# Eight heads of a gated delta network on one core: the turn of each head's result goes from TensorE to VectorE blocks and DRAM transfers

## The chip, the core and the metric

The kernel runs on one core of a Trainium2 chip. The metric is the device time of one execution in microseconds (us). Three runs of the kernel before took 2697.6, 2695.23 and 2692.07 us, median 2695.23.

## The reference, cut to what matters

One layer of a decoder: a prompt of 2048 tokens and 32 sample tokens, width 1024, all in float32. Of the two branches the change touches the second, a gated delta rule with 8 heads of 128 features:

```
h = layernorm(x) * (1 + scale) + shift
u_a, v_a, z_a, qkv, z_b, b_raw, a_raw, ga, gb = split(h @ w_in)
y_a   = chunk_gmlp(gelu(u_a), gelu(v_a), z_a, ...)        # branch A
q,k,v = split(silu(short_conv(qkv)))                      # branch B, per head
o, s  = gated_delta(l2norm(q), l2norm(k), v, g, beta, s0) # chunks of 64/128 tokens, a state S carried along
o     = rmsnorm(o) * onorm_g                              # over the 128 features of a head
y_b   = o * silu(z_b)
m     = sigmoid(ga) * (y_a @ w_pa) + sigmoid(gb) * (y_b @ w_pb)
x_new = layernorm(ALPHA * x + gate * (m @ w_o))           # gate comes from silu(c) @ w_ada
```

## The kernel before, in words

**Tiling.** The prompt goes in two halves of 1024 tokens (half 0 carries the sample tokens too). Each float32 product is made of three matmuls of split operands (high and low parts), so a group of 128 output features by 384, 288 or 512 tokens takes 24 matmuls. In each half the groups follow one another on TensorE: a small one for b and a, then per head k, q, v, z_b (and ga for the first six heads), then gb (8 groups), V (8), U and Z (16), the rest of ga, PA, PB and w_o. In half 1, V is made with tokens on the partitions (`v_tokens`): its weights go, split, into the eight Y tiles, which the heads use as buffers until then. `v_take` waits for the event `("headdone", 1, 7)`, the end of the last head, and then takes all of them.

**Side work of a head.** Beside the groups run, per head: the convolutions and norms of k, q and v, a Gram matrix, an inverse of unit triangular blocks (`inverse`, mostly GpSimd), a chain of 8 steps over the state (`chain`), and `o_out`, once for each 512 tokens (q = 0, 1). `o_out` takes the chain's result from PSUM with tokens on the partitions, works out its norm (ScalarE squares, a power on GpSimd), multiplies it into the buffer `ob` (VectorE), turns it by four TensorE transposes of 128x128 into PSUM (`pt`), multiplies it by gain and silu(z_b), which stand with features on the partitions (VectorE), and writes it to DRAM (`d_yb`).

**What sets the order.** A greedy planner in Python (`Sched`) runs when the program is built. Every piece of work is a stream that asks for an engine with a modelled duration, for a buffer of a role, or for an event; the planner takes the stream with the earliest modelled start and writes its instruction down. So the order on every engine is fixed before the run, and each engine works through its own list in order. All transfers go through one queue, SP. In the model a transfer ends at the earliest 2 us after its start, and longer with many short runs; consecutive `dma` calls in one stream that pass `dep=t` follow one another in the model.

**Buffers.** A head's small buffer `hs` and its `ZZ` have two copies; `chain` gives them back when both `("oq", half, h, q)` have been signalled, so head h+2 can start its k only after head h's last `d_yb` write. The inverse takes the role `Z`, two units of scratch, for three arrays Z1, Z2, Z3. In half 0 the gate of the layer (`ada_gate`) loads eight blocks of `w_ada` of 512 KB into buffers of the role `gw`, which lie in the same Y tiles as the heads' buffers, splits each into Y2R or Y3R in turn (ScalarE and VectorE) and multiplies it (six matmuls 9x512 each).

Of the kernel before, what the change touches and what calls it, by code (L numbers as in the profile page):

```python
# [13 lines left out]
P = 128  # L14
D = 1024
KT = 8
H = 8
# [152 lines left out]
def hybrid_step_kernel(ctx: ExitStack, tc: tile.TileContext, x_prompt, x_sample, state_conv, state_ssm,  # L170
# [15 lines left out]
    def const(n):  # L186
        o = cpos[0]
        cpos[0] += (n + 1) // 2 * 2
        assert cpos[0] <= NF, cpos[0] - NF
        return o  # L190
# [14 lines left out]
    def place(off):  # L205
        if off >= RO:
            return AR, off - RO, NF - RO
        if off >= WHL:
            return TW_, off - WHL, 4096
        if off >= YO:  # L210
            return ycur[(off - YO) // YT], (off - YO) % YT, YT
        return TX, off, 32 * UNIT
    PS = ps_pool.tile([P, 8, 512], F32, name="psum")[:]

    def V(off, *dims, p0=0, np_=P):
        dims = [[1, d] if isinstance(d, int) else list(d) for d in dims]
        t, o, st = place(off)
        return bass.AP(t.tensor, t.offset + p0 * st + o, [[st, np_]] + dims)

    def Q(bank, off, *dims, p0=0, np_=P):  # L220
        dims = [[1, d] if isinstance(d, int) else list(d) for d in dims]
        return bass.AP(PS.tensor, PS.offset + p0 * 4096 + bank * 512 + off, [[4096, np_]] + dims)

    def dram(name, n):
        return dr_pool.tile([1, n], F32, name=name)[:]

    def DV(t, off, *dims):
        return bass.AP(t.tensor, t.offset + off, [list(d) for d in dims])
# [3 lines left out]
    def role(name, cands):  # L232
        roles[name] = cands

    def xs_units(base, first, n):
        return tuple(range(base + first, base + first + n))
# [5 lines left out]
    def Yc(first, n):  # L242
        return (YO + first * UNIT, xs_units(32, first, n))

    def Rc(first, n):
        return (RO + first * UNIT, xs_units(64, first, n))
# [3 lines left out]
    role("KV", [Yc(16, 4), Yc(20, 4)])  # L250
    role("ZZ", [Yc(24, 2), Yc(26, 2)])
    role("U", [Yc(28, 2)])
    role("Z", [Yc(30, 2)])
    role("cp", [Rc(0, 2), Rc(2, 2)])
    role("cu", [Rc(4, 1)])
    role("kx", [Rc(5, 1)])
# [60 lines left out]
    S = Sched(98 + len(unit_names), roles)  # L317
# [11 lines left out]
    c_ong, c_negA, c_dtb = const(2), const(8), const(8)  # L329
# [10 lines left out]
    def SCR(**kw):  # L340
        return V(c_scr, P // 2, **kw).bitcast(BF16)
# [18 lines left out]

    d_v = {(half, h, i): dram(f"d_v{half}{h}{i}", n * P)
           for half, ns in enumerate(((384, 384, 256), (512, 512))) for h in range(H) for i, n in enumerate(ns)}


    def fsz(ap):
        n = 1
        for s in ap.shape[1:]:
            n *= s
        return n
# [7 lines left out]
    def dma(out, in_, dep=None, late=0.0):  # L377
        n = 1
        for s in out.shape:
            n *= s  # L380
        run = 4 * min(out.shape[-1], in_.shape[-1])
        t = yield ("o", "DMA", (n * 4 / 300.0 * max(1.0, 512.0 / run), late), dep)
        nc.sync.dma_start(out=out, in_=in_)
        return t

    def act(out, in_, func=AF.Copy, dep=None, scale=None, bias=None, accum=None):
        ns = fsz(out) / 1.2 + (55 if in_ps(in_) else 95)
        ns += 93 * (not isinstance(scale, (int, float, type(None)))) + 93 * (bias is not None) + 150 * (accum is not None)
        if func in (AF.Ln, AF.Exp, AF.Tanh, AF.Gelu_apprx_tanh):
            ns += 1300 * ((func == AF.Ln) != S.ln_table)  # L390
            S.ln_table = func == AF.Ln
        t = yield ("o", "ACT", ns, dep)
        kw = {}
        if scale is not None:
            kw["scale"] = scale
        if bias is not None:
            kw["bias"] = bias
        if accum is not None:
            kw["accum_out"] = accum
        nc.scalar.activation(out, in_, func, **kw)  # L400
        return t

    def dve_ns(out, ins, rate=1.0):
        return fsz(out) / (0.96 * rate) + (80 if any(in_ps(i) for i in ins) else 130)

    def tt(out, a, b, op, dep=None, eng="DVE"):
        if eng == "DVE":
            t = yield ("o", "DVE", dve_ns(out, (a, b)), dep)
            nc.vector.tensor_tensor(out=out, in0=a, in1=b, op=op)  # L409
        else:  # L410
            t = yield ("o", "POOL", 240 + 2.15 * fsz(out), dep)
            nc.gpsimd.tensor_tensor(out=out, in0=a, in1=b, op=op)  # L412
        return t
# [8 lines left out]
    def stt(out, a, s, b, op0, op1, dep=None):  # L422
        aps = not isinstance(s, (int, float))
        t = yield ("o", "DVE", dve_ns(out, (a, b)) + 60 * aps, dep)
        nc.vector.scalar_tensor_tensor(out=out, in0=a, scalar=s, in1=b, op0=op0, op1=op1)  # L425
        return t

    def vtrans(out, a, dep=None):

        t = yield ("o", "DVE", fsz(out) / 0.96 + 150, dep)  # L430
        nc.vector.transpose(out, a)  # L431
        return t
# [19 lines left out]
    def tp(out, in_, idn=None, dep=None):  # L452
        t = yield ("o", "PE", 109.0, dep)
        nc.tensor.transpose(out, in_, ident[: in_.shape[0], : in_.shape[0]] if idn is None else idn)  # L454
        return t
# [697 lines left out]
    def hd(half, h):  # L1153
        return heads.setdefault((half, h), {})
# [268 lines left out]
    def inverse(half, h, t):  # L1423
        me = hd(half, h)
# [3 lines left out]
        t = max(t, t0)  # L1428
# [9 lines left out]
        t = yield ("o", "DVE", 210.0, ub[2])  # L1438
        nc.vector.tensor_copy(V(T, 256), V(c_ti, 256))
        t = max(t, tw)  # L1440
        for j in range(31):
# [5 lines left out]
            t = yield from tt(tmp, arow, piv, ALU.mult, dep=t, eng=SUB)  # L1447
            t = yield from tt(dst, dst, tmp, ALU.subtract, dep=t, eng=SUB)
        S.release(wb, t)
        for cls in range(4):  # L1450
# [5 lines left out]
        t = yield ("o", "DVE", 340.0, tw)  # L1456
# [7 lines left out]
                           dep=max(tw, Ub[2]))  # L1464
# [4 lines left out]
                           bc(V(c_bd, [32, 2], [1, 32], **h64).unsqueeze(1), [64, 8, 2, 32]), ALU.mult, dep=max(t, t0))  # L1469

        Zb = yield ("a", "Z")
        Z1, Z2, Z3 = (Zb[0] + 256 * i for i in range(3))
        B = [dict(p0=32 * i, np_=32) for i in range(4)]


        pb = yield ("a", "pt")
        pc = yield ("a", "pu")
        t = yield ("o", "PE", 16 * 38.0 + 120, max(t, pb[2], pc[2], Zb[2]))
# [6 lines left out]
        t = yield ("o", "PE", 24 * 32.0 + 120, max(ta, tb))  # L1485
        for c in range(8):
            nc.tensor.matmul(Q(pb[0], 32 * c, 32, **B[1]), V(Uc + 32 * c, 32, **B[1]), V(Z1 + 32 * c, 32, **B[1]),  # L1487
                             start=True, stop=True)
            for a, q in ((2, pc), (0, pb)):
# [3 lines left out]
                           dep=max(t, t2))  # L1493
# [10 lines left out]
        pb = yield ("a", "pt")  # L1504
        t = yield ("o", "PE", 16 * 32.0 + 140, max(ta, pb[2]))
        for c in range(8):
# [5 lines left out]
                           dep=tc_)  # L1512
        t = yield from act(V(Z2, 256), Q(pb[0], 0, 256), dep=t)
        pc = yield ("a", "pu")
        t = yield ("o", "PE", 16 * 32.0 + 140, max(t, t3, pc[2]))
        for c in range(0, 8, 2):
            i = 64 * (c // 2)
# [6 lines left out]
        t = yield from ts(V(U + P + 64, [2 * P, 4], [1, 64], **h64), Q(pc[0], 0, [64, 4], [1, 64], **l64), -1.0,  # L1524
                          ALU.mult, dep=max(t, tb))
        S.release(pb, ta)
        S.release(pc, t)
        t = max(ta, t)
# [63 lines left out]
    def o_out(half, h, q, po, t):  # L1592
        me = hd(half, h)
        hs = me["hs"][0]
        te = t
        for i in range(4):
            t = yield from act(SCR(), Q(po[0], i * P, P), AF.Square, accum=V(hs + 56 + 4 * q + i, 1), dep=te)
        tn = 0.0
        for cgi in range(len(CG[half])):
            tn = max(tn, (yield ("w", ("nq", half, h, cgi))))  # L1600
        no, rs = V(hs + 56 + 4 * q, 4), V(hs + 64 + 4 * q, 4)
        t = yield from stt(no, no, 1.0 / P, V(hs + 48 + 4 * q, 4), ALU.mult, ALU.add, dep=max(t, tn))
        t = yield from pow_(rs, no, 0)
        ob = yield ("a", "ob")
        t = yield from tt(V(ob[0], [P, 4], [1, P]), Q(po[0], 0, [P, 4], [1, P]), bc(rs.unsqueeze(2), [P, 4, P]),
                          ALU.mult, dep=max(t, ob[2]))
        S.release(po, t)
        pb = yield ("a", "pt")
        for i in range(4):
            t = yield from tp(Q(pb[0], i * P, P), V(ob[0] + i * P, P), dep=max(t, pb[2]))  # L1610
        tz = 0.0
        for cgi in range(len(CG[half])):
            tz = max(tz, (yield ("w", ("zz", half, h, cgi))))
        t = yield from stt(V(ob[0], 512), Q(pb[0], 0, 512), V(c_ong, 1), V(me["ZZ"][0] + 512 * q, 512),
                           ALU.mult, ALU.mult, dep=max(t, tz))
        S.release(pb, t)
        t = yield from dma(DV(d_yb, h * P * TW + 512 * q, [TW, P], [1, 512]), V(ob[0], 512), dep=t)
        S.release(ob, t)
        S.signal(("oq", half, h, q), t)
        S.signal(("ybd", half, h, q), t + 500)  # L1620
# [568 lines left out]
    for half in range(2):  # L2189
# [54 lines left out]
        for cgi in range(len(CG[half]) if half == 0 else 1):  # L2244
            for g in range(KT):
# [3 lines left out]
                elif g > 1:  # L2249
                    keep = (XO + 4 * g * UNIT, lambda: ("done", last[(0, "pb")]), (P, TW))  # L2250
                q = add(w_o, D, g * P, half, P, hy, (lambda k, c, half=half: ("m", half, k, c)), o_sink(half, g), 1.0,
                        cgs=[cgi], pre=after_pb if cgi == 0 and g == 0 else None, keep=keep,
                        use=wo[g] if cgi else None)
# [81 lines left out]
```

## Time and profile before

| what | value |
|---|---|
| runs | 2697.6, 2695.23, 2692.07 us, median 2695.23 |
| profiled execution, its own time | 2690.44 us |
| its span in the trace | 2688.7 us |
| TensorE busy | 2641.5 us, 98% of the span |
| VectorE, ScalarE, GpSimd busy | 1479.2, 987.0, 555.9 us |
| transfers | 281.34 MB in 506976 packets |
| mean granted TensorE clock | 0.996 |

The page gives for each engine its busy time; 98% for TensorE says that the kernel is a nearly gapless row of matmuls. In the views below PE is TensorE, DVE is VectorE, ACT is ScalarE, POOL is GpSimd and SP is the queue that issues the transfers. "L449" is a line of the kernel; the same helper lines stand three lines lower (L452) in the changed one.

### The profile page before, as it was taken

How to read it: one execution, taken by the hardware profiler on the slowest of the kernel's cores; microseconds unless marked ns; L12 is line 12 of the kernel's file. 1: busy time of each engine (PE TensorE's matmuls, PEld its weight loads, DVE VectorE, ACT ScalarE, POOL GpSimd, SP SyncE). 2: the span in 40 equal slices, each digit the busy share in tenths (PEclk: the TensorE clock that was granted, in tenths of full speed). 3: DMA queues.
4: the chain of work that ended last, by engine and by line, in shares of the span. 5: the costliest groups of instructions: out<-in, count | busy, mean ns of one | idle time of the engine just before them, and what ended most of it. 6: DMA issues, size and time to landing. Idle time of an engine off the chain costs nothing. (4 is left out here: it accounts for less than half of the span.)

```text
span 2688.7 us, 43893 instructions
## 1 busy us (share of the span) xinstructions
PE 2641.5 (98%) x16250; PEld 2331.7 (87%) x16250; DVE 1479.2 (55%) x3247; ACT 987.0 (37%) x2650; POOL 555.9 (21%) x1452
## 2 busy tenths in 40 slices
PE   6999999999999999999999999999999999999998
PEld 4999989999899999999997788888888888888876
DVE  5676767777643364334547666666762323433446
ACT  5554545455332222221325444444442312221120
POOL 2054544334300000000001434444350000000001
PEclk9999999999999999999999999999999999999999
DMA  6232343333675462332523333333233322233332
GB/s 217 69 91 74 102 110 90 87 82 82 174 193 109 101 202 71 101 118 83 164 78 108 83 88 94 93 85 92 73 80 101 113 92 77 77 116 98 111 121 86
DMA packets 506976, 281.34 MB, mean 105 GB/s; under 512 B 210025, under 2 KB 471457, under 8 KB 506762
## 3 DMA queue, kind: packets, MB, share of 16 engines
q1 hardware_dynamic: 506762, 278.55, 36.9%
q8 instruction: 127, 2.08, 0.3%
q14 instruction: 87, 0.71, 0.1%
HBM read 210.03 MB, written 68.43 MB: 104 GB/s over the span
## 5 line engine op out<-in xcount | busy, mean ns | idle before, releaser
L449 PE MATMUL psum<-TX,TWHL 128*128 128x384 f32 (+3 forms) x9296 | 1959.4, 359 | 9.3 <-DVE TX L409 5.9
L449 PEld LDWEIGHTS psum<-TX,TWHL 128*128 128x128 f32 (+1 forms) x9296 | 1556.3, 188 | 163.8 <-DVE TX L409 7.0
L400 ACT ACTIVATE arena<-psum 128x128 bf16<-128x128 f32 (+9 forms) x888 | 299.4, 346 | 719.7 <-PE psum L449 596.8
L438 POOL TENSOR_TENSOR arena<-arena 128x4 f32<-128x4 f32 (+4 forms) x139 | 121.2, 874 | 1592.3 <-DVE arena L419 1380.7
L425 DVE SCALAR_TENSOR_TENSOR arena<-arena 128x512 f32<-128x512 f32 (+9 forms) x633 | 348.9, 560 | 91.2 <-ACT arena L400 79.6
L412 POOL TENSOR_TENSOR arena<-arena 128x60 f32<-128x60 f32 (+24 forms) x992 | 352.1, 355 | 174.7 <-DMA d_v<-arena 36.9
L409 DVE TENSOR_TENSOR TWHL<-arena,TWHL 128x512 fp32r<-128x512 f32 (+1 forms) x344 | 233.2, 687 | 198.3 <-ACT TWHL L400 196.1
L425 DVE SCALAR_TENSOR_TENSOR arena<-arena,psum 128x128 f32<-128x128 f32 (+3 forms) x342 | 132.7, 404 | 357.2 <-PE psum L449 246.6
L400 ACT ACTIVATE TWHL<-arena 128x512 fp32r<-128x512 f32 x344 | 213.6, 627 | 240.3 <-PE psum L449 117.0
L400 ACT ACTIVATE arena<-arena 128x128 f32<-128x128 f32 (+9 forms) x513 | 234.7, 493 | 130.4 <-DVE arena L425 86.2
L409 DVE TENSOR_TENSOR arena<-arena 128x1024 f32<-128x1024 f32 (+12 forms) x251 | 108.6, 438 | 9.6 <-DMA arena<-in_lnv_g_dram 5.6
L454 PE MATMUL psum<-arena 128*128 128x128 f32 (+8 forms) x381 | 93.6, 269 | 2.6 <-ACT Y3F L400 0.8
L400 ACT ACTIVATE Y7F<-psum 32x256 f32<-32x256 f32 (+6 forms) x115 | 46.5, 405 | 117.8 <-DVE Y7F L431 37.5
L1226 POOL COPY arena<-arena 128x3 f32<-128x3 f32 x120 | 37.4, 312 | 233.2 <-ACT arena L400 232.8
L425 DVE SCALAR_TENSOR_TENSOR arena<-psum,arena 128x512 f32<-128x512 f32 (+4 forms) x72 | 36.9, 528 | 84.2 <-PE psum L449 84.0
L400 ACT ACTIVATE TX<-arena 128x512 fp32r<-128x512 f32 (+2 forms) x84 | 46.9, 586 | 89.3 <-DMA arena<-d_yb 72.2
L400 ACT ACTIVATION_READ_ACCUMULATOR arena<-psum 128x1 f32 x392 | 76.5, 195 | 0.0
L419 DVE TENSOR_SCALAR arena<-arena 128x3 f32<-128x3 f32 (+8 forms) x247 | 54.4, 224 | 36.3 <-ACT arena L400 24.2
L449 PEld LDWEIGHTS psum<-arena 128*128 128x128 f32 (+3 forms) x364 | 55.2, 171 | 17.1 <-issue 7.0
L454 PEld LDWEIGHTS psum<-arena 128*128 128x128 f32 (+8 forms) x381 | 49.7, 136 | 22.8 <-issue 12.0
L449 PE MATMUL psum<-arena 128*128 128x128 f32 (+5 forms) x364 | 66.5, 269 | 1.2 <-ACT arena L400 1.0
L409 DVE TENSOR_TENSOR TX<-arena,TX 128x512 fp32r<-128x512 f32 (+2 forms) x84 | 52.1, 639 | 21.7 <-ACT TX L400 21.5
(249 smaller groups left out, 2706.2 us busy)
## 6 DMA issues: line engine op xcount, KB each, us to landing
arena<-in_w_in_dram SPq DMA_DIRECT2D x288, 256.0 KB
out_dram<-arena SPq DMA_DIRECT2D x25, 512.0 KB
arena<-in_x_prompt_dram SPq DMA_DIRECT2D x24, 512.0 KB
arena<-d_gc SPq DMA_DIRECT2D x16, 512.0 KB
arena<-d_blk SPq DMA_DIRECT2D x64, 128.0 KB
d_yb<-arena SPq DMA_DIRECT2D x32, 256.0 KB
d_vh<-arena SPq DMA_DIRECT2D x16, 512.0 KB
arena<-d_vh SPq DMA_DIRECT2D x16, 512.0 KB
```

What stands on the lines that cost most here:

```text
L400: nc.scalar.activation(out, in_, func, **kw)
L409: nc.vector.tensor_tensor(out=out, in0=a, in1=b, op=op)
L412: nc.gpsimd.tensor_tensor(out=out, in0=a, in1=b, op=op)
L419: nc.vector.tensor_scalar(out=out, in0=a, scalar1=s1, scalar2=s2, op0=op0, **kw)
L425: nc.vector.scalar_tensor_tensor(out=out, in0=a, scalar=s, in1=b, op0=op0, op1=op1)
L438: nc.gpsimd.tensor_tensor(out=out, in0=a, in1=e, op=ALU.pow)
L449: nc.tensor.matmul(out, lhsT, rhs, start=start, stop=stop)
L454: nc.tensor.transpose(out, in_, ident[: in_.shape[0], : in_.shape[0]] if idn is None else idn)
L1226: nc.gpsimd.tensor_copy(V(c_tail + gi, [24, 3]), V(x0 + n0, 3))
```

## The change: o_out of every head but the last of half 1

For 30 of the 32 calls of `o_out` (all but half 1, head 7), the four TensorE transposes are replaced. VectorE transposes `ob` within blocks of 32x32 into a new buffer `obt` (one instruction, 128x512); four transfers of 64 KB write the four bands of 32 partitions to a new DRAM array `d_o`, in runs of 128 B, so that block (i, j) lands at place (j, i); a fifth transfer of 256 KB reads it back into `ob`. The multiplication by gain and z_b then takes its first operand from `ob` in place of PSUM. The unit for `obt` is the second one of the role `Z`; Z1 and Z2 of the inverse now share a place.

```diff
-    role("Z", [Yc(30, 2)])
+    role("Z", [Yc(30, 1)])
+    role("obt", [Yc(31, 1)])
...
+    d_o = {(half, h, q): dram(f"d_o{half}{h}{q}", 512 * P) for half in range(2) for h in range(H) for q in range(2)}
...
-        Z1, Z2, Z3 = (Zb[0] + 256 * i for i in range(3))
+        Z1, Z2, Z3 = Zb[0], Zb[0], Zb[0] + 256
...
         S.release(po, t)
-        pb = yield ("a", "pt")
-        for i in range(4):
-            t = yield from tp(Q(pb[0], i * P, P), V(ob[0] + i * P, P), dep=max(t, pb[2]))
         tz = 0.0
         for cgi in range(len(CG[half])):
             tz = max(tz, (yield ("w", ("zz", half, h, cgi))))
-        t = yield from stt(V(ob[0], 512), Q(pb[0], 0, 512), V(c_ong, 1), V(me["ZZ"][0] + 512 * q, 512),
+        src, pb = V(ob[0], 512), None
+        if (half, h) == (1, H - 1):
+            pb = yield ("a", "pt")
+            src = Q(pb[0], 0, 512)
+            for i in range(4):
+                t = yield from tp(Q(pb[0], i * P, P), V(ob[0] + i * P, P), dep=max(t, pb[2]))
+        else:
+
+            bt = yield ("a", "obt")
+            t = yield from vtrans(V(bt[0], 512), src, dep=max(t, bt[2]))
+            d = d_o[half, h, q]
+            for i in range(4):
+                t = yield from dma(DV(d, 32 * i, [512, 32], [P, 4], [32 * 512, 4], [1, 32]),
+                                   V(bt[0], [P, 4], [32, 4], [1, 32], p0=32 * i, np_=32), dep=t)
+            S.release(bt, t)
+            t = yield from dma(src, DV(d, 0, [512, P], [1, 512]), dep=t)
+        t = yield from stt(V(ob[0], 512), src, V(c_ong, 1), V(me["ZZ"][0] + 512 * q, 512),
                            ALU.mult, ALU.mult, dep=max(t, tz))
-        S.release(pb, t)
+        if pb is not None:
+            S.release(pb, t)
         t = yield from dma(DV(d_yb, h * P * TW + 512 * q, [TW, P], [1, 512]), V(ob[0], 512), dep=t)
```

Since the planner works from these durations, the change also moves instructions elsewhere. At three places the order reads as follows.

TensorE at the end of the heads of half 1, before: `psum<-TX,TWHL` are matmuls of the projections (here of gb), `psum<-arena,Y5F` and `Y3F` the last links of head 7's chain, `psum<-arena` at L454 the four transposes of its last `o_out`, and `Y0R,TX` is where `v_tokens` begins.

```order
L449 MATMUL psum<-TX,TWHL 128x512 x4
L449 MATMUL psum<-arena,Y5F 128x128
L449 MATMUL psum<-arena,Y3F 128x128
L449 MATMUL psum<-TX,TWHL 128x512 x19
L454 MATMUL psum<-arena 128x128
L449 MATMUL psum<-TX,TWHL 128x512 x3
L454 MATMUL psum<-arena 128x128
L449 MATMUL psum<-TX,TWHL 128x512 x3
L454 MATMUL psum<-arena 128x128
L449 MATMUL psum<-TX,TWHL 128x512 x3
L454 MATMUL psum<-arena 128x128
L449 MATMUL psum<-TX,TWHL 128x512 x96
L449 MATMUL psum<-Y0R,TX 128x512 x3
```

The same place in the changed kernel:

```order
L452 MATMUL psum<-TX,TWHL 128x512 x4
L452 MATMUL psum<-arena,Y7F 128x128
L452 MATMUL psum<-arena,Y5F 128x128
L452 MATMUL psum<-arena,Y3F 128x128
L457 MATMUL psum<-arena 128x128 x4
L452 MATMUL psum<-Y0R,TX 128x512 x3
```

The 124 matmuls of gb that stood between the chain's last link and `v_tokens` now all stand ahead of the chain's end; only the four transposes are left between the two.

TensorE in the V stage of half 0, before (`Y2R,Y4R` and `Y3R,Y4R` with 9x512 are `ada_gate`'s matmuls, one buffer each; the others are V's projections):

```order
L449 MATMUL psum<-TX,TWHL 128x384 x18
L449 MATMUL psum<-Y3R,Y4R 9x512
L449 MATMUL psum<-TX,TWHL 128x384 x3
L449 MATMUL psum<-Y3R,Y4R 9x512
L449 MATMUL psum<-TX,TWHL 128x384 x3
```

and the part of the changed kernel where they stand closest:

```order
L452 MATMUL psum<-TX,TWHL 128x384 x9
L452 MATMUL psum<-Y3R,Y4R 9x512 x6
L452 MATMUL psum<-Y2R,Y4R 9x512 x3
L452 MATMUL psum<-TX,TWHL 128x384 x3
...
L452 MATMUL psum<-TX,TWHL 128x384 x15
L452 MATMUL psum<-Y3R,Y4R 9x512 x6
L452 MATMUL psum<-Y2R,Y4R 9x512 x6
L452 MATMUL psum<-Y3R,Y4R 9x512 x4
L452 MATMUL psum<-TX,TWHL 128x288 x3
```

Before, three or four projection matmuls stood between two of the gate's, and 18 to 31 between two buffers; now buffers follow one another with none between.

ScalarE at the same place in the changed kernel (`Y2R<-Y5F` and `Y3R<-Y5F` are the high parts of the gate's weights, `Y7F<-psum` the gelu of V, `TWHL<-arena` the split of the next projection weights, `Y0F` and `Y1F` normalise token rows of half 1):

```order
L403 ACTIVATE Y1F<-Y1F,arena 128x1024
L403 ACTIVATE Y2R<-Y5F 128x1024
L403 ACTIVATE Y3R<-Y5F 128x1024
L403 ACTIVATE TWHL<-arena 128x512 x2
L403 ACTIVATE Y2R<-Y5F 128x1024
L403 ACTIVATE Y7F<-psum 128x384
L403 ACTIVATE Y3R<-Y5F 128x1024
L403 ACTIVATE Y0F<-Y0F,arena 128x1024
L403 ACTIVATE Y2R<-Y5F 128x1024
L403 ACTIVATE Y1F<-Y1F,arena 128x1024
L403 ACTIVATE Y3R<-Y5F 128x1024
```

All eight splits now stand behind the first gelu of V; before, six of them stood ahead of it and two behind.

## Rows read from the trace of the kernel before

**Rows 1.** The page's head and its parts 1 and 2: the span, busy time and share of each engine, and busy tenths in 40 slices of 67.2 us (TensorE).

```profile
span 2688.7 us, 43893 instructions
PE 2641.5 (98%) x16250; PEld 2331.7 (87%) x16250; DVE 1479.2 (55%) x3247; ACT 987.0 (37%) x2650; POOL 555.9 (21%) x1452
...
PE   6999999999999999999999999999999999999998
...
```

**Rows 2.** Busy time of each engine in stretches (from:to, length, then PE, PEld, DVE, ACT, POOL, granted clock, share and rate of transfers). 200:820 is the heads of half 0, gb and the start of V; 820:1200 the rest of V, U and Z; 1560:2100 the heads of half 1 and gb.

```profile
200.00:820.00 620.00, 619.10 (x4672) 574.57 (x4671) 423.20 (x1080) 290.68 (x938) 231.57 (x625) 1.00 0.42 111
820.00:1200.00 380.00, 377.04 (x2342) 372.07 (x2341) 158.81 (x308) 92.94 (x186) 6.29 (x10) 1.00 0.43 117
1560.00:2100.00 540.00, 539.07 (x3431) 444.68 (x3430) 318.91 (x664) 242.13 (x732) 200.44 (x518) 1.00 0.33 89
```

**Rows 3.** The view of waits, TensorE, from 60 us to the end: what it waited for, us in total, times, longest.

```profile
PE psum L449 <- DVE TX L409: 6.9, 3, 5.2
PE psum L449 <- ACT Y7F L400: 2.4, 1, 2.4
```

**Rows 4.** Timeline of TensorE at the end of head 7, half 1 (start us, length, instruction, count; in square brackets idle time before it).

```profile
2072.86 0.39 PE L449 MATMUL psum<-arena,Y3F 128*128 128x128 f32 x2
2073.01 4.69 PE L449 MATMUL psum<-TX,TWHL 128*128 128x512 f32 x19
2077.53 0.27 PE L454 MATMUL psum<-arena 128*128 128x128 f32 x1
2077.56 0.94 PE L449 MATMUL psum<-TX,TWHL 128*128 128x512 f32 x3
2078.34 0.27 PE L454 MATMUL psum<-arena 128*128 128x128 f32 x1
...
2079.98 22.64 PE L449 MATMUL psum<-TX,TWHL 128*128 128x512 f32 x96
2102.46 0.86 PE L449 MATMUL psum<-Y0R,TX 128*128 128x512 f32 x3
```

**Rows 5.** Timeline of VectorE after the chain's end in half 1: the last `o_out` (2076.17 and 2080.26) and the low parts of `v_tokens`' weights (Y0R to Y7R).

```profile
2076.17 0.69 DVE L409 TENSOR_TENSOR arena<-psum,arena 128x512 f32<-128x512 f32 x1 [1.12 <-POOL arena L438]
2080.26 0.75 DVE L425 SCALAR_TENSOR_TENSOR arena<-psum,arena,Y6F 128x512 f32<-128x512 f32 x1 [3.40 <-PE psum L454]
2082.13 0.28 DVE L409 TENSOR_TENSOR Y0R<-arena,Y0R 128x128 fp32r<-128x128 f32 x1
...
2098.91 0.29 DVE L409 TENSOR_TENSOR Y7R<-arena,Y7R 128x128 fp32r<-128x128 f32 x1
```

**Rows 6.** A load of half a group of those weights: the issue on SP, and the split on ScalarE that waited for it.

```profile
2087.21 2.33 SPq L383 DMA_DIRECT2D arena<-in_w_in_dram  x3
...
2090.14 0.31 ACT L400 ACTIVATE Y4R<-arena 128x128 fp32r<-128x128 f32 x1 [1.68 <-DMA arena<-in_w_in_dram]
```

**Rows 7.** TensorE's two gaps over 2 us outside the kernel's start: the row that follows each, and the stretches behind them (columns as in rows 2).

```profile
848.58 1.75 PE L449 MATMUL psum<-TX,TWHL 128*128 128x384 f32 x7 [2.38 <-ACT Y7F L400]
1432.22 1.07 PE L449 MATMUL psum<-TX,TWHL 128*40 128x512 f32 x2 [5.21 <-DVE TX L409]
...
849.60:853.00 3.40, 3.40 (x12) 3.40 (x11) 0.26 (x1) 0.00 (x0) 0.00 (x0) 0.51 0.51 77
1430.00:1436.70 6.70, 3.76 (x9) 1.86 (x10) 6.41 (x10) 2.26 (x4) 0.38 (x1) 0.50 0.02 7
```

**Rows 8.** Groups of VectorE instructions by line and shape (count, busy us, mean ns, idle before).

```profile
L431 DVE STREAM_TRANSPOSE arena<-arena 128x512 f32<-128x512 f32 x16 | 11.3, 707 | 0.2
L425 DVE SCALAR_TENSOR_TENSOR arena<-psum,arena,Y6F 128x512 f32<-128x512 f32 x32 | 24.0, 750 | 32.2 <-PE psum L454 32.1
L425 DVE SCALAR_TENSOR_TENSOR arena<-arena 128x512 f32<-128x512 f32 x180 | 132.6, 738 | 40.8 <-ACT arena L400 38.6
```

**Rows 9.** The nearest path of the same kind, v through DRAM (`d_v` is written in four transfers, then read back): the waits of the queue SP and of VectorE for it, the sizes, and the page's part 3 for the queue.

```profile
SPq L383 <- DMA d_v<-arena: 35.7, 23, 4.1
...
DVE Y4F L409 <- DMA Y4F<-d_v: 11.6, 5, 7.3
...
DVE Y5F L409 <- DMA Y5F<-d_v: 4.0, 6, 1.1
...
d_v<-arena SPq DMA_DIRECT2D x64, 64.0 KB
...
q1 hardware_dynamic: 506762, 278.55, 36.9%
```

**Rows 10.** The V stage of half 0: the gate's splits on ScalarE (first and last of eight), the first gelu of V, the low part on VectorE, and a 512 KB load from its issue to the instruction that waited for it.

```profile
767.41 1.05 ACT L400 ACTIVATE Y2R<-Y5F 128x1024 fp32r<-128x1024 f32 x1
...
808.95 0.49 ACT L400 ACTIVATE Y7F<-psum 128x384 f32<-128x384 f32 x1 [0.99 <-PE psum L449]
...
818.69 1.05 ACT L400 ACTIVATE Y3R<-Y5F 128x1024 fp32r<-128x1024 f32 x1
...
768.50 1.23 DVE L409 TENSOR_TENSOR Y2R<-Y5F,Y2R 128x1024 fp32r<-128x1024 f32 x1
...
787.22 1.27 SPq L383 DMA_DIRECT2D Y0F<-in_x_prompt_dram  x1
...
791.90 0.70 DVE L736 BATCH_NORM_STATS2 arena<-Y0F 128x6 f32<-128x512 f32 x1 [3.36 <-DMA Y0F<-in_x_prompt_dram]
```

## The prediction, on record before the changed kernel ran

> **What bounds the kernel now.** I read the page's head and slices first: TensorE is busy 98% of the span, and its only weak slice is the first [rows 1]. The table by stages says the same where the change is made: in the heads of half 0 TensorE is idle 0.9 of 620 us, in those of half 1 0.9 of 540, while VectorE is at 68% and 59%, GpSimd at 37% and transfers at 42% and 33% [rows 2]. The view of waits finds hardly any stall: 6.9 us for TX in three places and one of 2.4 us [rows 3]. So TensorE's list sets the time. A change can win only by shortening that list, and it loses by every hole it tears into it.
>
> **The transposes that go.** 30 calls times 4 is 120 transposes. The recorded 0.27 us overlaps the next matmul. From one transpose to the next with three matmuls between it is 2078.34 - 2077.53 = 0.81 us; a matmul of that shape takes (2102.46 - 2079.98) / 96 = 0.234 us, three of them 0.70 [rows 4]. That leaves 0.11 us, and 120 x 0.11 = 13.2 us of saving.
>
> The page TensorE: Matmul & The Clock Gate of the Trainium skill, section Part 4: PE-mode transpose, gives about 275 ns for one in a kernel. By that figure the saving would be an estimated 33 us. The recorded length, 0.27 us, agrees with it, but the starts around it do not, and they decide.
>
> **What takes their place.** A block transpose of 128x512 on VectorE takes 0.71 us, 30 of them 21 us; the multiplication by z_b costs as much from SBUF (738 ns) as from PSUM (750) [rows 8]. VectorE rises from 55 to 56%. With a third of its time free in the heads this is hidden; bare, it would be the whole 21 us.
>
> The 150 transfers (30 x 512 KB = 15.7 MB, 5.6% more) have a like in `d_v`, four writes of mostly 64 KB and a read back. There SP stood 35.7 us in 23 places for the writes, 1.55 us each, and VectorE stood 15.6 us in 11 of the 40 reads [rows 9]. For 30 reads that makes 47 us on SP and 11.7 on VectorE. Behind SP's wait stand mostly weight loads, and three buffers hold weights ahead of a group, which lasts 48 x 0.234 = 11.2 us in half 1. TensorE is idle 1.8 us in both head stages in spite of the 40 `d_v` paths [rows 2]. I therefore charge it 0.8 us; the bounds are 0 and 11.7.
>
> That Z1 and Z2 share a place costs nothing: the inverse writes Z2 when Z1's readers are done, mostly GpSimd sets its pace, and TensorE has other work meanwhile. Without that cover it would be a short wait in each of 16 inverses.
>
> **What is late next: the heads.** In the planner's model five chained transfers, at least 2 us each, stand where four transposes took 0.4. `hs` and `ZZ` of head h come free only behind them, and head h+2 waits for `hs`. The order shows the result: counted in matmuls at their own lengths, head 7's chain starts some 46 us later in half 0 and 30 us later in half 1. The planner fills the time with later groups, so TensorE doesn't stop inside the heads; but at each half's end the cover is spent. That is where the costs lie.
>
> **End of the heads in half 1.** Before, head 7's chain ends on TensorE at C = 2073.0, and 124 matmuls of gb lie between it and `v_tokens` at 2102.46: 29.4 us of work [rows 4]. In the new order only four transposes are left. `v_tokens` needs weights in Y tiles that the last head holds, so TensorE must stand. Step by step from C: squares, the power on GpSimd and the product end 2076.86 - 2073.0 = 3.9 us later [rows 5]; four transposes with nothing between, 0.27 for one and 0.11 for each other with a little for the hand-over, bring C + 4.7; the multiplication of 0.75 us brings C + 5.5 [rows 5]. Then eight half loads of 256 KB must be split. Three raw buffers can hold loads already; the first splits run to about C + 6.7 (four of 0.28 us). A reload takes 2090.14 - 2087.21 = 2.9 us [rows 6], so the next arrive at C + 9.6, and a second round, another split and another load, at about C + 13.6. A high and a low part make C + 14.3 the start of `v_tokens`. Less 0.5 us for the four transposes, which are work in both, 13.8 us are idle. It could be 12, with splits and loads meshing better; or 25.9, the time that it took before from C to 2098.9 [rows 5], when the splits queued behind evictions of gb. I take the step count, since those evictions are gone from the place.
>
> Behind a gap the clock falls. After 2.38 us without work a stretch of 3.4 us ran at 0.51, and after 5.2 us one of 6.7 us, with 3.76 busy, at 0.50 [rows 7]: 1.2 GHz instead of 2.4. Half of 3.4 and of 3.76 is lost, 1.7 to 1.9 us; I add 1.9.
>
> **The gate in the V stage of half 0.** The gate's eight blocks use the last heads' Y tiles. Before, their splits ran from 767.41 to 818.69, 7.3 us apart, six of them before V's first gelu [rows 10], with projections between all matmuls. Now all eight stand behind that gelu, and 9 and 16 gate matmuls stand in a row. One buffer is held for a load of 4.7 us (787.22 to 791.90) and splits of 1.05 and 1.23 [rows 10], 7.0 in all; two are in turn (the third holds the bias row), so a block can come every 3.5 us. 16 matmuls are 2.7 blocks: 9.3 us, less 16 x 0.234 = 3.7 for themselves and about 2.6 for the 15 projections ahead of them; 3.0 idle. 9 matmuls are 1.5 blocks: 5.3 less 2.1 and 1.6; 1.6 idle. With something for the ends I take 5 us. The bounds are 0, if loads run ahead, and 20: the old pace, 4.2 blocks x 7.3 = 31 less 11 of work.
>
> **The sum.** -13.2 + 13.8 + 1.9 + 5 + 0.8 = +8.3 us. On the profiled execution's own time, 2690.4, that is 2698.7. The median of the runs stands 4.8 us above that execution, so I predict a median of 2703.
>
> **The rivals.** A change of 0.2%, 5.4 us, is about what a measurement of this kernel can tell from none.
>
> *Faster: only the list gets shorter.* If the weights of `v_tokens` were ready when the chain ends and the gate ran ahead, -13.2 + 2 would give 2684. For it speaks that TensorE hides every side path now [rows 2]; against it, that `v_take` waits for the last head's end. It decides once gap, clock and gate together stay below 8 us. Chance 0.08.
>
> *Faster: a transpose costs its recorded length.* 120 x 0.27 = 32 us saved against 21.5 us of cost gives 2685. Against it stand the starts [rows 4]. Its rule is in the section of the Trainium skill named above. Chance 0.04.
>
> *No change.* The gap at 12 us and its clock against the saving, the gate without a stall: -13.2 + 12 + 1.9 + 0.8 = +1.5, about 2697. That the gate's loads could run ahead speaks for it; the rows without projections between speak against. Chance 0.22.
>
> *Slower by more: the gap is 25.9 us.* If SP and ScalarE serve the splits as slowly as before, the sum is +20.4, 2716. Against it, the evictions that slowed them are gone. Chance 0.13.
>
> *Slower by more: the reads through DRAM are waited for.* If TensorE pays the 11.7 us of VectorE's waits, the sum is +19, 2714. The even busy shares of the heads [rows 2] speak against. Chance 0.08. The page VectorE: DVE Perf Modes of the Trainium skill, section Rules for kernel authors, advises TensorE for a 128x128 transpose where a PSUM destination will do, as it does here. By that rule the change loses; no row before shows a head's path in the new form.
>
> **How the numbers follow.** The forecast has 0.45, its own range 2697 to 2709; a small part of that, 0.06, falls within 0.2% of before. Faster: 0.08 + 0.04 = 0.12. Same: 0.22 + 0.06 = 0.28. Slower: 0.39 + 0.13 + 0.08 = 0.60. The range reaches down to 2688, which leaves out most of the two faster cases, and up to 2724, the two slow rivals partly together; about 0.2 is left out.
>
> **What would show it.** Right: TensorE's chain of gb runs without holes to head 7's last link in half 1, then a gap of 12 to 16 us, named as waits for the last `o_out` and for splits of Y0R, with a granted clock near 0.5 behind it; in the V stage of half 0 waits of TensorE for Y2R and Y3R of some 5 us; TensorE's busy time lower by about 13 us, and the heads still at 99% or more. Wrong: busy time lower by 30 us (the transposes were dearer than their starts say); a gap of 25 us; waits of TensorE inside the heads for weights (TWHL) behind SP's stands for `d_o`, or for v and k behind VectorE's; no stall in the V stage. The term that I know least is the gate's, then the gap.

## The result: slower, and the profile after

The changed kernel took 2711.09 us (median of 4 runs, 2709.74 to 2715.68) against 2693.65 of the kernel before beside it (2690.96 to 2697.6): 17.4 us more, a ratio of 1.0066 with a 95% interval of 1.0053 to 1.0078. The forecast was slower, 2703 in a range of 2688 to 2724. The direction held and the time lies in the range, but the loss is twice the 8.3 us of the sum, and it lies above the 2697 to 2709 that the forecast kept for its own mechanism.

The page's head and parts 1 and 2 of the kernel after:

```profile
span 2712.2 us, 43935 instructions
PE 2643.9 (97%) x16130; PEld 2328.8 (86%) x16130; DVE 1502.1 (55%) x3277; ACT 989.4 (36%) x2650; POOL 583.4 (22%) x1452
...
PE   6999999999998999999999999999999899999998
PEclk8999999999998999999999999999999899999999
...
q1 hardware_dynamic: 574442, 294.29, 39.7%
```

There are 120 matmul records fewer, and two weak slices of TensorE that weren't there [rows 1], at about 815 to 880 and 2100 to 2170 us. In both the granted clock dips too. TensorE's busy time didn't fall, since a matmul at the slow clock is busy for longer.

Its view of waits, TensorE, the longest first (kernel's start left out):

```profile
PE psum L452 <- ACT Y0R L403: 8.9, 1, 8.9
...
PE psum L452 <- DVE TX L412: 7.0, 3, 5.4
...
PE psum L452 <- ACT arena L403: 4.4, 7, 1.4
PE psum L457 <- DVE arena L412: 4.2, 2, 3.7
PE psum L452 <- ACT Y3R L403: 3.0, 1, 3.0
PE psum L452 <- ACT Y2R L403: 2.3, 1, 2.3
PE psum L457 <- POOL arena L1229: 1.8, 1, 1.8
PE psum L452 <- ACT Y7F L403: 1.8, 2, 1.1
PE psum L452 <- DVE Y2R L412: 1.3, 1, 1.3
```

Of these, the waits for TX and one for Y7F stood there before [rows 3], and three for ACT arena:

```profile
PE psum L449 <- ACT arena L400: 1.7, 3, 1.0
```

New are Y0R and L457 <- DVE arena, the place before `v_tokens`, and Y2R and Y3R, the gate in the V stage of half 0. The first place: TensorE's timeline, then stretches (length, PE, PEld, DVE, ACT, POOL, granted clock, share and rate of transfers), then two splits on ScalarE:

```profile
2109.01 0.49 PE L452 MATMUL psum<-arena,Y5F 128*128 128x128 f32 x2 [0.63 <-ACT arena L403]
2109.33 0.39 PE L452 MATMUL psum<-arena,Y3F 128*128 128x128 f32 x2
2113.39 1.11 PE L457 MATMUL psum<-arena 128*128 128x128 f32 x4 [3.67 <-DVE arena L412]
2123.39 1.65 PE L452 MATMUL psum<-Y0R,TX 128*128 128x512 f32 x3 [8.89 <-ACT Y0R L403]
...
2128.65 0.86 PE L452 MATMUL psum<-Y4R,TX 128*128 128x512 f32 x3
...
2114.30:2123.30 9.00, 0.20 (x1) 0.00 (x0) 5.16 (x22) 3.19 (x15) 0.00 (x0) 0.50 0.55 150
2123.30:2127.00 3.70, 3.61 (x9) 2.89 (x10) 2.40 (x11) 2.15 (x11) 0.00 (x0) 0.50 0.52 138
...
2119.03 0.31 ACT L403 ACTIVATE Y4R<-arena 128x128 fp32r<-128x128 f32 x1 [2.80 <-DMA arena<-in_w_in_dram]
...
2123.03 0.31 ACT L403 ACTIVATE Y0R<-arena 128x128 fp32r<-128x128 f32 x1 [1.35 <-DMA arena<-in_w_in_dram]
```

The chain ends at about 2109.5. The transposes start 3.9 us behind it, the first reloaded weights are split at 9.5 us, the last that `v_tokens` waits for at 13.5, and `v_tokens` starts at 13.9. That is step by step what was forecast (3.9, 9.6, 13.6 and 14.3); before, 29 us of gb lay there [rows 4]. Behind the hole 12 matmuls take 2128.65 - 2123.39 = 5.26 us in place of 12 x 0.234 = 2.81: 2.5 us are lost at the granted 0.50, which is 1.2 GHz.

The V stage of half 0, timeline and stretches:

```profile
834.03 1.54 PE L452 MATMUL psum<-Y3R,Y4R 128*9 128x512 f32 x6
837.92 0.68 PE L452 MATMUL psum<-Y2R,Y4R 128*9 128x512 f32 x2 [2.34 <-ACT Y2R L403]
839.94 1.88 PE L452 MATMUL psum<-Y2R,Y4R 128*9 128x512 f32 x4 [1.35 <-DVE Y2R L412]
844.83 1.02 PE L452 MATMUL psum<-Y3R,Y4R 128*9 128x512 f32 x2 [3.01 <-ACT Y3R L403]
...
840.00:844.00 4.00, 1.82 (x4) 0.31 (x4) 1.90 (x6) 1.41 (x2) 0.55 (x1) 0.50 0.78 174
844.00:848.00 4.00, 2.75 (x7) 1.00 (x8) 2.70 (x3) 2.04 (x3) 0.00 (x0) 0.50 0.67 90
848.00:852.00 4.00, 4.00 (x17) 3.61 (x15) 1.22 (x1) 0.09 (x1) 0.00 (x0) 0.50 0.94 214
```

The row of 16 gate matmuls is where TensorE stands, as the order said. With the smaller stalls around it (1.1 at 829, then 0.4, 0.4 and 0.7 up to 862) it makes 9.3 us idle, where before 3.0 were [rows 2]. And 8.6 us of busy time run at 0.50, so 4.3 us are lost, against about 1.7 behind the gap of before [rows 7].

The heads themselves (first row half 0, second row half 1) lose little:

```profile
200.00:820.00 620.00, 617.80 (x4682) 577.39 (x4681) 429.15 (x1096) 289.23 (x941) 248.67 (x630) 1.00 0.47 117
1560.00:2100.00 540.00, 537.72 (x3396) 442.58 (x3395) 324.69 (x647) 236.46 (x697) 214.91 (x533) 1.00 0.39 100
```

TensorE is idle 2.2 and 2.3 us there, against 0.9 and 0.9 [rows 2]. The new path's own rows, on VectorE and SP:

```profile
L434 DVE STREAM_TRANSPOSE Y7F<-arena 128x512 f32<-128x512 f32 x30 | 21.1, 702 | 0.1
...
DVE arena L428 <- DMA arena<-d_o: 4.7, 5, 1.3
...
SPq L386 <- DMA d_o<-Y7F: 36.5, 22, 3.9
```

VectorE works the forecast 21 us. It waits 4.7 us for the reads, where 11.7 was forecast, and SP stands 36.5 us in 22 places, where 47 was forecast, a stand for each of the 30 reads. TensorE's view of waits has no entry for a transfer.

### The profile page after: what moved, and what is told of

Same layout as the page of the kernel before. It is cut to its first block, busy times and chain, and to the rows that moved or that the text cites. A ratio compares the mean times of both kernels' runs of the same rounds, so it can differ in the third digit from the quotient of the medians.

```text
span 2712.2 us, 43935 instructions
## 1 busy us (share of the span) xinstructions
PE 2643.9 (97%) x16130; PEld 2328.8 (86%) x16130; DVE 1502.1 (55%) x3277; ACT 989.4 (36%) x2650; POOL 583.4 (22%) x1452
## 3 DMA queue, kind: packets, MB, share of 16 engines
q1 hardware_dynamic: 574442, 294.29, 39.7%
## 5 line engine op out<-in xcount | busy, mean ns | idle before, releaser
L403 ACT ACTIVATE arena<-psum 128x128 bf16<-128x128 f32 (+10 forms) x891 | 300.2, 347 | 713.1 <-PE psum L452 601.2
L441 POOL TENSOR_TENSOR arena<-arena 128x1 f32<-128x1 f32 (+4 forms) x139 | 119.0, 857 | 1572.8 <-DVE arena L422 1308.0
L415 POOL TENSOR_TENSOR arena<-arena 128x60 f32<-128x60 f32 (+24 forms) x992 | 385.3, 388 | 216.3 <-DMA d_v<-arena 43.4
L428 DVE SCALAR_TENSOR_TENSOR arena<-arena 128x512 f32<-128x512 f32 (+11 forms) x636 | 349.6, 562 | 89.7 <-ACT arena L403 77.8
L403 ACT ACTIVATE arena<-arena 128x128 f32<-128x128 f32 (+8 forms) x513 | 234.3, 493 | 149.4 <-DVE arena L428 95.1
L412 DVE TENSOR_TENSOR arena<-arena 128x3 f32<-128x3 f32 (+11 forms) x254 | 111.5, 442 | 10.2 <-DMA arena<-in_lnv_g_dram 5.2
L428 DVE SCALAR_TENSOR_TENSOR arena<-psum,arena 128x512 f32<-128x512 f32 (+4 forms) x72 | 36.9, 528 | 82.7 <-PE psum L452 81.1
L422 DVE TENSOR_SCALAR arena<-arena 128x4 f32<-128x4 f32 (+8 forms) x247 | 54.2, 223 | 47.6 <-ACT arena L403 36.1
L1211 POOL COPY arena<-arena 128x3 f32<-128x3 f32 x120 | 36.5, 304 | 172.5 <-DVE Y0F L428 67.6
L457 PE MATMUL psum<-arena 128*128 128x128 f32 (+7 forms) x261 | 64.8, 288 | 6.9 <-DVE arena L412 4.2
L1229 POOL COPY arena<-arena 128x3 f32<-128x3 f32 x120 | 36.2, 303 | 159.4 <-ACT arena L403 158.9
```

The costliest lines, as they stand in the source:

```text
L422: nc.vector.tensor_scalar(out=out, in0=a, scalar1=s1, scalar2=s2, op0=op0, **kw)
L441: nc.gpsimd.tensor_tensor(out=out, in0=a, in1=e, op=ALU.pow)
L1211: nc.gpsimd.tensor_copy(V(x0, 3), V(c_tail + gi, [24, 3]))
L1229: nc.gpsimd.tensor_copy(V(c_tail + gi, [24, 3]), V(x0 + n0, 3))
```

## Experiments

All comparisons are with the kernel before, run beside them. They ran in three groups (e1 to e4, e5 to e8, e9 to e12), in which its median was 2693.89, 2691.11 and 2692.15 us; so times of different groups are compared by their ratios. Differences in us below are the ratio times that median, and the medians' own differences lie within 1.5 us of them. Two theories were set against each other. **Late heads**: the planner believes that `hs` comes back late, plans each half's last heads later, and TensorE meets their ends without cover. **Load of the path**: the block transposes and transfers slow the kernel by themselves.

**e1, the transposes alone.**

```diff
-            t = yield from tp(Q(pb[0], i * P, P), V(ob[0] + i * P, P), dep=max(t, pb[2]))
+            if last_head:
+                t = yield from tp(Q(pb[0], i * P, P), V(ob[0] + i * P, P), dep=max(t, pb[2]))
+            else:
+                t = yield ("o", "PE", 109.0, max(t, pb[2]))
```

> The kernel before, with the 120 transposes (all but those of half 1, head 7) planned but not issued, and nothing in their place: the multiplication by z_b takes the unturned result, so the heads' results are left unturned. It prices the transposes alone. If one costs what the starts around it say (0.11 us): 13 us faster than before. If it costs its recorded length (0.27 us): 32 us faster. If it is hidden behind the weight loads: no change.

2679.77 us, ratio 0.9948 (0.9931 to 0.9964): 14.1 us faster by the medians, 0.117 us for each transpose, in an interval of 9.7 to 18.6 us. The spans of the two profiled executions, 2688.7 and 2677.8, differ by 10.9, or 0.09 us for each. The starts give its price; the recorded length would have given 32. With this order it is also about the most that a replacement of the transposes could win.

**e2 and e3, one half at a time.**

```diff
-        if (half, h) == (1, H - 1):
+        if half == 1:                       # e2
+        if half == 0 or h == H - 1:         # e3
```

> The change in half 0 alone. Theory (late heads): the V stage of half 0 keeps its stalls for the gate's splits, the gap before v_tokens is gone: about 3 us slower than before. Rival (the path through VectorE and DRAM costs by itself, evenly per call): 16 of 30 calls, so 16/30 of 17 us = 9 us slower.

2698.08 us, ratio 1.0010 (1.0001 to 1.0020): 2.7 us slower. Its view of waits keeps the gate's in the V stage (2.9 us for Y3R, 2.5 for Y2R) and has none for Y0R.

> The change in half 1 alone. Theory (late heads): the gap of 12 to 13 us before v_tokens and its slow clock stay, the V stage of half 0 is as before: about 15 us slower than before. Rival (the path costs by itself): 14 of 30 calls, 8 us slower.

2706.12 us, ratio 1.0042 (1.0028 to 1.0055): 11 us slower. The loss isn't even per call: 14 calls cost about four times as much as 16. Half 1 has the hole, at the same place and of the same size:

```profile
2108.34 0.66 PE L457 MATMUL psum<-arena 128*128 128x128 f32 x4 [3.67 <-DVE arena L412]
2117.91 1.65 PE L452 MATMUL psum<-Y0R,TX 128*128 128x512 f32 x3 [8.90 <-ACT Y0R L403]
```

**e4, hs back after its last reader.** The whole path is kept.

```diff
         S.release(po, t)
+        S.signal(("hq", half, h, q), t)      # o_out, behind the multiplication by the norm
...
         for q in range(2):
-            e = max(e, (yield ("w", ("oq", half, h, q))))
+            e = max(e, (yield ("w", ("hq", half, h, q))))
         S.release(me["hs"], e)
+        for q in range(2):
+            e = max(e, (yield ("w", ("oq", half, h, q))))
```

> The changed kernel, but the head's small buffer hs goes back as soon as its last reader, the multiplication by the norm, is done, and no longer behind the write to d_yb. Theory (late heads): in the order 27 us of gb stand again between the chain's end and v_tokens, and the gate's matmuls are spread out again; the gap before v_tokens and most of the V stage's stalls go, and the saving of the transposes shows: about 10 us faster than before (8 to 13). Rival (the path costs by itself, by VectorE's, SP's or the transfers' load): those 150 transfers and 30 block transposes are all still there, so 10 us or more slower than before.

2693.12 us, ratio 0.9996 (0.9987 to 1.0006): no different from before. The whole loss is gone with every transfer and block transpose still in place. But the expectation was 10 us faster than before, and it missed that by 9. The hole before `v_tokens` is gone; what TensorE now waits for:

```profile
PE psum L452 <- ACT Y7F L403: 6.9, 2, 5.9
...
PE psum L457 <- ACT arena L403: 1.8, 2, 1.0
PE psum L457 <- DVE Y0F L428: 1.5, 1, 1.5
PE psum L457 <- DVE arena L412: 1.1, 2, 0.7
```

One stall in the V stage, for V's gelu, of 5.9 us where before 2.4 were [rows 3], and several of about 1 us in the heads.

**e5 and e6, what remains of the loss in e4: the path or the order?** The order of e4 is kept to the instruction and parts of the path are planned but not issued.

```diff
-            t = yield from vtrans(V(bt[0], 512), src, dep=max(t, bt[2]))
+            t = yield ("o", "DVE", 512 / 0.96 + 150, max(t, bt[2]))          # e5 only
...
-                t = yield from dma(DV(d, 32 * i, ...), V(bt[0], ...), dep=t)
+                t = yield ("o", "DMA", (32 * 512 * 4 / 300.0 * 4.0, 0.0), t)  # e5 and e6
...
-            t = yield from dma(src, DV(d, 0, [512, P], [1, 512]), dep=t)
+            t = yield ("o", "DMA", (P * 512 * 4 / 300.0, 0.0), t)             # e5 and e6
+            src = V(bt[0], 512)                                               # e6 only
```

> The kernel of e4, its order kept to the instruction, but neither VectorE's 30 block transposes nor the 150 transfers issued: the multiplication by z_b takes the unturned result, so the heads' results are left unturned. Theory A (what is left of the loss is the path's own load on VectorE, SP and the transfers): about 10 us faster than e4, 2683. Theory B (what is left is the order, which still differs from before): the same as e4, 2693.

2687.92 us, ratio 0.9986 (0.9976 to 0.9996).

> As e5, but VectorE's block transposes are issued and only the 150 transfers are not: the heads' results are turned within blocks of 32 alone. If the transfers (SP's issues and waits, VectorE's wait for the read) are the load that counts: as fast as e5, within 2 us. If VectorE's 21 us count: as slow as e4.

2687.09 us, ratio 0.9988 (0.9979 to 0.9997). Between e4 and e5 lie 0.10%, 2.7 us, and their intervals just overlap; e6, as fast as e5, shows no share of VectorE's either. Theory B (the order) is much nearer: without any path the kernel wins 3.8 us of the 14, and its trace still shows the stall of the V stage, at the same size:

```profile
849.40 2.93 PE L452 MATMUL psum<-TX,TWHL 128*128 128x384 f32 x8 [5.94 <-ACT Y7F L403]
```

In the heads the traces do part the two. With the same order TensorE is idle 5.7 and 2.3 us in e4 (first two rows) and 4.1 and 0.3 in e5, so in this order the path costs it 3.6 us there:

```profile
200.00:820.00 620.00, 614.29 (x4631) 571.18 (x4632) 423.56 (x1089) 288.04 (x937) 245.79 (x628) 1.00 0.48 122
1560.00:2100.00 540.00, 537.74 (x3406) 442.78 (x3405) 328.65 (x672) 239.04 (x724) 206.40 (x534) 1.00 0.41 103
...
200.00:820.00 620.00, 615.92 (x4645) 573.31 (x4642) 415.39 (x1075) 290.99 (x941) 244.19 (x627) 1.00 0.41 110
1560.00:2100.00 540.00, 539.72 (x3407) 445.54 (x3406) 320.26 (x665) 241.23 (x734) 205.24 (x528) 1.00 0.34 91
```

**e7, a shorter path in the model too.** e4, and the four writes no longer planned one behind the other.

```diff
+            tv = t
             for i in range(4):
                 t = yield from dma(DV(d, 32 * i, [512, 32], [P, 4], [32 * 512, 4], [1, 32]),
-                                   V(bt[0], [P, 4], [32, 4], [1, 32], p0=32 * i, np_=32), dep=t)
+                                   V(bt[0], [P, 4], [32, 4], [1, 32], p0=32 * i, np_=32), dep=tv)
```

> The kernel of e4, and in the planner the four writes to d_o may all start when the block transpose is done, not each behind the one before; the hardware's waits are the same. The model then sees the path some 6 us shorter. Theory (late heads): the order has no row of gate matmuls left and the same 26 us of gb ahead of v_tokens; the V stage's stalls shrink: 2 to 5 us faster than e4. Rival (load of the path): no more than 2 us from e4.

2681.17 us, ratio 0.9966 (0.9953 to 0.9979): 9 us faster than before and 8 faster than e4, more than the expected 2 to 5; the interval overlaps that of e1, which has no turn at all. The same 30 block transposes and 150 transfers run; only the order differs. Its longest wait outside the kernel's start but for TX, and its two head stages:

```profile
PE psum L452 <- ACT Y7F L403: 4.6, 1, 4.6
...
200.00:820.00 620.00, 619.41 (x4672) 574.70 (x4669) 432.00 (x1101) 291.14 (x945) 242.82 (x630) 1.00 0.49 124
1560.00:2100.00 540.00, 539.94 (x3399) 445.38 (x3398) 326.60 (x681) 242.32 (x738) 198.38 (x516) 1.00 0.40 105
```

In the heads TensorE is idle 0.6 us of 620 and 0.1 of 540, less than before, at transfer shares of 49% and 40% in place of 42% and 33% [rows 2]. So in this order the load isn't felt in the heads. That Z1 and Z2 share a place is in e7 as well.

**e8, more cover.** Groups 6 and 7 of ga stand ahead of V in both halves, on top of e7.

```diff
+        for g in (6, 7):                     # behind gb, ahead of V
+            win(half, OFF_GA + g * P, ga_early_sink(half, g))
```

> The kernel of e7, and the groups 6 and 7 of ga stand ahead of V in both halves (they stood behind U and Z), 22 us more of projections between the last head and V. Theory (holes where the cover is spent): the gate's blocks are through before V's first gelu and the V stage's wait shrinks: 3 to 6 us faster than e7. Rival (load of the path): as e7.

2681.39 us, ratio 0.9961 (0.9948 to 0.9975): as e7. The expectation of 3 to 6 us missed, though the wait that it was about did shrink, from 4.6 us to two of 1.0:

```profile
PE psum L452 <- ACT Y7F L403: 2.0, 2, 1.0
```

From the first projection matmul to the end the two profiled executions take the same, 2628.3 us in e7 and 2627.8 in e8, so the gain went elsewhere: new in e8 are waits of 1.0 us for Y1F and 0.8 for TWHL, and the two groups now go through DRAM, 4.3 MB more. Which of these took it up isn't shown.

**e9, the control.** The edit of e4 on the kernel before.

> The kernel before, transposes on TensorE, with nothing but the earlier return of hs as in e4: the control for e4 and e7. The heads of before were not late, and TensorE has hardly a hole in them: no change, within 3 us of before. If the earlier return is worth something by itself, it is faster by 5 us or more, and e7 owes that to it.

2690.49 us, ratio 0.9994 (0.9985 to 1.0004): no change. So e7 doesn't owe its gain to the earlier return alone; what is left is the transposes that went.

**e10, the hole alone.** The changed kernel with its late heads, and in half 1 alone the two ga groups moved between gb and `v_tokens`.

> The changed kernel with its late heads, and in half 1 alone the groups 6 and 7 of ga moved ahead of v_tokens: 21 us of projections stand between the last head's chain and v_tokens. It prices the hole there. Theory: the gap of 12.6 us and the slow clock behind it go, 14 to 16 us faster than the changed kernel, so 1 to 4 us slower than before. Rival (the weights of v_tokens are late for another reason than the last head): the gap stays, no gain.

2694.44 us, ratio 1.0012 (1.0002 to 1.0021): 0.54% or 14.5 us faster than the changed kernel, as expected. The stalls in the V stage of half 0 are still there; of the hole this is left:

```profile
2130.49 1.07 PE L452 MATMUL psum<-Y0R,TX 128*128 128x512 f32 x3 [1.48 <-ACT Y0R L403]
```

**e11, unchained writes alone**, with `hs` returned late.

> The changed kernel with the planner's four writes unchained, as in e7, but hs returned late, as in the change. In the order 18 us of gb cover the last head in half 1 and one row of five gate matmuls is left. Theory (the length of the modelled path sets how late the heads are): the gap before v_tokens goes, since 14 us are needed there; 0 to 8 us faster than before. Rival (hs must come back early): 10 us or more slower than before.

2695.81 us, ratio 1.0010 (1.0001 to 1.0020): 2.7 us slower than before. Nothing but the model's durations changed, and most of the loss is gone. But the expectation missed here too: 18 us of cover don't close a hole of 14. `v_tokens` starts 23.1 us behind the chain's end (2082.6) in place of 13.9, since ScalarE's list has evictions of gb between the splits, and it stood 4.7 us for one of them (second row):

```profile
2105.76 1.65 PE L452 MATMUL psum<-Y0R,TX 128*128 128x512 f32 x3 [4.72 <-ACT Y0R L403]
...
2095.47 0.60 ACT L403 ACTIVATE arena<-psum 128x512 f32<-128x512 f32 x1 [4.71 <-PE psum L452]
```

**e12, heads 6 and 7 back to TensorE's transposes**, on top of e7.

> The kernel of e7, with heads 6 and 7 of both halves back on TensorE's transposes. Their 28 transposes cost 3 us; theirs were the d_o transfers that fell into the V stage of half 0. If those make the 4.6 us stall that e7 still has there: 0 to 3 us faster than e7. If not: 3 us slower than e7.

2682.81 us, ratio 0.9963 (0.9948 to 0.9978): as e7. The stall in the V stage is down from 4.6 to before's 2.4 us, which about pays the transposes that came back. These are 24 and not 28 (16154 matmul records against e7's 16130), since the last head of half 1 had never left TensorE; by e1 they cost 2 to 3 us. Whether the transfers or the order made the stall smaller isn't shown:

```profile
843.90 1.85 PE L452 MATMUL psum<-TX,TWHL 128*128 128x384 f32 x9 [2.43 <-ACT Y7F L403]
```

## Why the prediction held in direction and was half the size

**The transposes' price**: 13.2 forecast; 14.1 measured by the medians of e1, 10.9 by its profiled execution against that of before. The rival with the recorded length falls. So does the estimate of 33 us from the 275 ns of the page TensorE: Matmul & The Clock Gate of the Trainium skill, section Part 4: PE-mode transpose.

**The hole before `v_tokens`**: 13.8 forecast; the trace has 3.67 + 8.89, and 0.63 ahead of the chain's last links, 13.2 in all. e10 gives it and its clock 14.5 us. The count of reloads was the right model, and the two reloads landed when it said; the bound of 25.9 was not reached, as no evictions of gb stood in the way, and e11, where some do, shows what they cost. That the hole comes from late heads, and these from the planner's view of the path and of `hs`, is shown by e4, which gives `hs` back earlier, and by e11, which shortens the path in the model alone.

**The clock behind it**: 1.9 forecast, 2.5 measured.

**The gate in the V stage** is the term that was mis-sized. The place, the rows of gate matmuls and the waits for Y2R and Y3R came as forecast. But I put 5 us; the idle time there rose by 6.3 (9.3 less 3.0), and the clock that fell in it, for which I charged nothing at this place, cost 4.3 against 1.7 before: together about 9.

**Stalls in the heads**: 0.8 forecast; 1.3 in half 0 and 1.4 in half 1. The longest, 1.8 us, stands in half 1 at 1978, and about 1.3 us go to a clock near 0.8 behind it. The rival of VectorE waiting 11.7 us for the reads falls: it waited 4.7, and e7 has the same reads with idle times under before's.

With the measured terms, all from profiled executions: -10.9 + 13.2 + 2.5 + 6.3 + 2.6 + 2.7 + 1.3 = 17.7 us. The medians differ by 17.4, in an interval of 14.3 to 21.0; with e1's 14.1 the sum would be 14.5. The spans differ by 23.5 us, but 5.3 of it stand already at the first projection matmul, and 18.2 are left. Up to there the order on TensorE is the same (before in the first row, the changed kernel in the second):

```profile
0.00:49.16 49.16, 25.67 (x159) 12.77 (x159) 26.18 (x82) 27.71 (x43) 14.77 (x48) 0.97 0.80 277
0.00:54.41 54.41, 31.98 (x158) 17.27 (x159) 26.54 (x82) 28.63 (x45) 14.81 (x48) 0.81 0.72 252
```

The other three runs of the changed kernel took 4.3 to 5.9 us less than the profiled one, and e4, with the same start, reaches that matmul at 50.0. So I count the 5.3 us as the spread of single executions.

One sign of being right didn't come: TensorE's busy time was to be 13 us lower and is 2.4 higher. The transposes did go, but 6.3 us of busy time were added ahead of the first projection, where the clock was lower, and 6.4 behind the stops (2.5 + 2.6 + 1.3).

That the time lies in the range owes something to luck. Its upper part was there for the two slow rivals, and neither came.

The rule of the page VectorE: DVE Perf Modes of the Trainium skill, section Rules for kernel authors, to turn 128x128 on TensorE where PSUM will do, gave the right direction for the change as written: it lost 17.4 us. e7, which differs in the early return of `hs` and in the model of the writes alone, shows the other sign, by 9 us: TensorE is busy 98% of its span, and its heads show no holes for VectorE or the transfers.

## What to carry to other kernels

Where an order is planned ahead, a step that lasts longer in the model costs little where it stands and much at the next place where the cover runs out: follow the buffers that it holds to that place and count the work left over it. Give a buffer back behind its last reader, not behind the end of the stream that holds it, before judging a change that lengthens the stream. Price a pipelined instruction by the starts around it, and best by a run that keeps the plan and leaves it out. Before the spans of two profiled executions are subtracted, compare them at an early landmark.

## What the runs showed of the hardware

A hole cost its length and then about 2 to 2.5 us more of TensorE at 0.50, whether it was one of 12.6 us (5.26 us for 12 matmuls worth 2.81) or e4's of 5.94, behind which 3.96 busy us ran at half speed (the first fence below). Several short stops in a row held the clock down for longer. In the changed kernel's V stage no single one is longer than 3.01 us, yet the clock stays at 0.50 from 840 to 852, with TensorE busy 1.82, 2.75 and then the full 4.00 us of each 4. The one of 1.83 us at 1978 was followed by four us at a mean of 0.77 as well. Stretches of e4 and of the changed kernel:

```profile
852.00:856.00 4.00, 3.96 (x12) 3.96 (x13) 0.48 (x1) 0.49 (x1) 0.00 (x0) 0.50 0.66 98
```

```profile
1980.00:1984.00 4.00, 4.00 (x15) 3.15 (x14) 2.39 (x5) 0.46 (x2) 3.37 (x9) 0.77 0.41 101
```

The kernel's first 50 us are not the same from one execution to the next. The fourteen profiled executions reach the first projection matmul between 49.1 us (e12) and 56.3 (e8), at granted clocks of 0.97 and 0.79 up to there. Counted from that matmul, e1 without any turn and e7 with the whole path take 2628.6 and 2628.3 us, and before 2639.5.

And 7.9 MB more written in runs of 128 B, and the same read back, took the queue's share from 36.9% [rows 9] to 39.7%. In e7, which moves the same, TensorE's heads lose nothing by it.
